# A decoder step with a dense and a gathered expert layer: six gather buffers, values through the weights' ring, and more value products of layer 1 as three float32r products

## The chip, the core and the metric

The kernel runs on one core of a Trainium2 chip. The metric is the device time in microseconds of one execution. Five engines run their own queues of instructions in order: PE (TensorE, products into PSUM), DVE (VectorE), ACT (ScalarE), POOL (GpSimd, here the issuer of gathers), and SP (SyncE, here the issuer of all other loads and stores).

## What is computed

One step of a two-layer decoder for 512 prompt tokens (four tiles of 128, called 0 to 3) and 8 sample tokens (called tile 4). Layer 0 is a gated MLP, layer 1 differential attention; each is followed by PEER, a layer of 16384 experts, which has most of the work:

```
s = einsum('thcd,hcnd->thcn', q, keys)          # 8 heads, 2 halves, 128 keys each
sv, si = top_k(s, 16)                           # then the best 16 of the 16 x 16 sums
act = gelu(einsum('thkd,td->thk', u_tab[eidx], h))
x  += einsum('thk,thkd->td', softmax(top_s) * act, v_tab[eidx])
```

So each token takes 128 rows (1024 float32 each) of the table u and 128 rows of the table v, for each of the two layers.

## The kernel before

The tokens of each layer are shared out in two ways. Two tiles are **gathered**: for each of 128 places of a token list POOL issues an indirect load of 128 rows (512 KB) into a buffer `gath` of the pool `gb` (line 706), and DVE multiplies it with h and sums (u rows, L715), or adds it, scaled, to x (v rows, L722). That is 512 gathers and 512 products of DVE per layer. The other two tiles, 256 tokens, are **dense**: `dense_peer` runs through all 16384 experts, 128 at a time, in four quarters of 32 blocks. Tiles 0 and 1 are dense in layer 0 and gathered in layer 1; 2 and 3 the other way round.

For a quarter q, `acts(q)` loads 32 blocks of u (`ub`, 512 KB each, from the ring `wt` of the pool `wp`, four buffers, which also holds all weights), and PE makes the activations W. In quarter 0 these are float32 products; later each block is split: `split` has ACT copy a rounded float32r part (`wh`, L209) and DVE make the rest (`wl`, L211), and three float32r products (hi hi, hi lo, lo hi: L488, L489, L491) take the place of one float32 product. `gates(q)` builds one-hot tiles (`ohj`, by ACT, L526 and L529, or by DVE, L520; `gi`, by DVE), has PE multiply them into `ps_g` (L533) and DVE multiply the result into W (L536), 16 times a quarter. Then the value blocks: for each of 32 blocks a load `vb` of 512 KB and PE adds W times v to four PSUM tiles y, by four float32 products (L576) or, in quarter 3 of both layers, by twelve float32r products (L572 to L574); for those v is split as above (with the tiles of `split`), and W as well (`wdh` by ACT, L565; `wdl` by DVE, L567, both in the buffers of `ohj`). The float32 blocks load v into three buffers of their own (tag `vb`), those of quarter 3 into the ring `wt`. The loop over the value blocks of quarter q draws `acts(q + 2)` (eight blocks in each of the first NV = 4 steps) and `gates(q + 1)` (in the other 28); `acts(1)` is drawn during `gates(0)`.

The order of instructions on every engine is set by a scheduler when the program is built. The products with gathered rows are held by `tick` and `pace`: the n-th may stand no earlier than the n-th of a list of named instructions of the dense work of the same layer. So gathered and dense work run side by side, through the front of a layer (projections, top 16, attention) and its dense stage. Before layer 1 goes on with tiles 2, 3, 1 and 4, the gathers of layer 0 must have ended, since tiles 2 and 3 are the gathered ones; its first part takes tile 0 alone.

`s_k` is the buffer for the scores of a tile in the first group of a layer, from which DVE ranks the 16 best.

Of the kernel before, what the change touches and what calls it, by code (L numbers as in the profile page):

```python
# [8 lines left out]
F32 = mybir.dt.float32  # L9
FR = mybir.dt.float32r  # L10
# [8 lines left out]
D = 1024  # L19
# [16 lines left out]
def body(ctx: ExitStack, tc: tile.TileContext, a):  # L36
# [3 lines left out]
    per = ctx.enter_context(tc.tile_pool(name="per", bufs=1))  # L40
    gb = ctx.enter_context(tc.tile_pool(name="gb", bufs=5))
    ks = ctx.enter_context(tc.tile_pool(name="ks", bufs=2))
    wp = ctx.enter_context(tc.tile_pool(name="wp", bufs=4))
# [425 lines left out]
    def dense_peer(layer, dpa, open_rest, open_odd, smp):  # L469
# [3 lines left out]
        NQ, QI, NV = 4, 32, 4  # L473
        J_DVE = [[1, 0, 0, 0], [1, 1, 1, 1]]
        V3 = [[3], [3]]
        W = {}
# [65 lines left out]
        dpb, py = open_rest()  # L542
# [9 lines left out]
        for q in range(NQ):  # L552
            na, ng = (na if not q else acts(q + 1), gates(q + 1)) if q + 1 < NQ else (iter(()), iter(()))
            for il in range(QI):
                i = q * QI + il
                w = W[q][:, il, :]
                r0 = layer * NE + i * 128
                three = q in V3[layer] and (il >= NV or q == NQ - 1)
                v = wp.tile([128, D], F32, name="vb", tag="wt") if three else \
                    dpa.tile([128, D], F32, name="vb", tag="vb", bufs=3)  # L560
                SY.dma_start(v, a["peer_v"][r0:r0 + 128, :])
                if three:
                    vh, vl = [z.rearrange("p c e -> p (c e)") for z in split(v.rearrange("p (c e) -> p c e", c=8), 0)]
                    wh = dpb.tile([128, 256], FR, name="wdh", tag="ohj", bufs=4)
                    SC.activation(wh, w, AF.Copy)  # L565
                    wl = dpb.tile([128, 256], FR, name="wdl", tag="ohj", bufs=4)
                    V.tensor_tensor(wl, w, wh.bitcast(F32), op=OP.subtract)  # L567
# [24 lines left out]
    def peer_front(tiles, n, layer, ph):  # L592
# [32 lines left out]
        sall = {}  # L625
# [6 lines left out]
        for sp in range(4):  # L632
# [10 lines left out]
            for t in tiles:  # L643
                c0 = col(t)
                if t < 4:
                    s = sall[t][:, sp] if sall else wk.tile([128, 4, 128], F32, name="s_k", tag="s_k", bufs=2)
                    ps = pm.tile([128, 4, 128], F32, name="ps_s", tag="mm")
# [30 lines left out]
    def sample_finish(pss, st, layer):  # L678
        state = st.pop()
        s = wk.tile([64, 1, 2, 128], F32, name="s_s", tag="s_k", bufs=2)  # L680
        for c in range(2):
# [88 lines left out]
    def run_layer(layer, setup):  # L770
# [36 lines left out]

        dpa = pool(fs, "dpa", "left", bufs=1)
        dense_peer(layer, dpa, open_rest, open_odd, st[4])
        gathers(st, layer)  # L810
        rs.close()
# [394 lines left out]
```

## Time and profile before

| | |
|---|---|
| unprofiled, median of 3 runs | 3254.13 us (3252.62 to 3262.15) |
| profiled execution | 3267.74 us, span 3266.0 us |
| PE busy | 2997.8 us, 92% of the span |
| DVE busy | 2424.0 us, 74% |
| ACT busy | 1382.3 us, 42% |
| DMA | 976.54 MB, 299 GB/s on average |

An engine's busy time is the time in which at least one of its instructions runs. PE overlaps a product with the next, so its busy time is not a measure of how well it is used. In time: layer 0's front to about 690 us (its gathers from about 190), its dense stage to 1570, layer 1's front to about 2436 (its gathers from about 1790), its dense stage to the end.

### The profile page before, as it was taken

How to read it: one execution, taken by the hardware profiler on the slowest of the kernel's cores; microseconds unless marked ns; L12 is line 12 of the kernel's file. 1: busy time of each engine (PE TensorE's matmuls, PEld its weight loads, DVE VectorE, ACT ScalarE, POOL GpSimd, SP SyncE). 2: the span in 40 equal slices, each digit the busy share in tenths (PEclk: the TensorE clock that was granted, in tenths of full speed). 3: DMA queues.
4: the chain of work that ended last, by engine and by line, in shares of the span. 5: the costliest groups of instructions: out<-in, count | busy, mean ns of one | idle time of the engine just before them, and what ended most of it. 6: DMA issues, size and time to landing. Idle time of an engine off the chain costs nothing.

```text
span 3266.0 us, 50065 instructions
## 1 busy us (share of the span) xinstructions
PE 2997.8 (92%) x18048; PEld 2237.3 (69%) x18048; DVE 2424.0 (74%) x5095; ACT 1382.3 (42%) x3156; POOL 1334.2 (41%) x1061
## 2 busy tenths in 40 slices
PE   7998979889899999978898988688799999999999
PEld 7898646788458758646787643455689658757757
DVE  1489779679776776679725788869989887686685
ACT  2344021256583593583353233321237433363444
POOL 0036662024555454455300556534334455354340
PEclk9999989999999999989999988699899999999999
DMA  7678987468999899889955989777778999989885
GB/s 247 230 280 308 336 318 244 149 225 304 386 345 365 319 350 373 313 306 373 351 168 189 361 311 324 253 266 239 284 275 308 340 364 361 328 314 355 329 306 165
DMA packets 271563, 976.54 MB, mean 299 GB/s; under 512 B 30938, under 2 KB 31770, under 8 KB 271306
## 3 DMA queue, kind: packets, MB, share of 16 engines
q0 software_dynamic: 152064, 553.72, 46.9%
q1 hardware_dynamic: 119250, 419.62, 36.1%
q8 instruction: 142, 2.33, 0.3%
q14 instruction: 107, 0.88, 0.1%
HBM read 966.76 MB, written 6.46 MB: 298 GB/s over the span
## 4 chain that ended last, share of the span: by engine, by line
PE 53%; DVE 13%; issue 12%; DMA 11%; POOL 7%; ACT 4%; another core or an unknown queue 0%; SPq 0%; POOLq 0%; DVEq 0%; ACTq 0%
PE y L576 13%; PE ps_d L231 7%; POOL gath L706 7%; PE ps_a L494 6%; PE ps_a L488 5%; PE ps_a L489 5%; PE ps_a L491 4%; DMA gath<-peer_v,ix 4%; DMA gath<-peer_u,ix 3%; PE ps_g L533 3%; DVE x L722 2%; ACT ohj L526 2%; DVE si L369 2%; DVE gath L715 2%; PE y L573 1%
## 5 line engine op out<-in xcount | busy, mean ns | idle before, releaser
L706 POOL DMA_INDIRECT gath<-peer_u,ix x512 | 651.5, 1272 | 947.4 <-DVE ix L674 355.5
L706 POOL DMA_INDIRECT gath<-peer_v,ix x512 | 644.8, 1259 | 718.2 <-DVE x L722 381.3
L722 DVE SCALAR_TENSOR_TENSOR x<-gath,act,x 128x1024 f32<-128x1024 f32 x512 | 655.6, 1281 | 70.3 <-DMA gath<-peer_v,ix 59.7
L576 PE MATMUL y<-vb,W 128*128 128x512 f32 x1536 | 703.4, 604 | 0.9 <-DMA vb<-peer_v 0.9
L715 DVE SCALAR_TENSOR_TENSOR gath<-gath,h_g 128x1024 f32<-128x1024 f32 x512 | 615.6, 1221 | 95.3 <-DMA gath<-peer_u,ix 94.0
L526 ACT ACTIVATE ohj<-iota,selJ 128x128 f16<-128x128 f32 x1408 | 426.0, 389 | 166.9 <-PE ps_g L533 152.8
L576 PEld LDWEIGHTS y<-vb,W 128*128 128x128 f32 x1536 | 283.3, 193 | 301.9 <-issue 299.2
L231 PE MATMUL ps_d<-hT,wt 128*128 128x128 f32 (+3 forms) x2048 | 433.6, 371 | 26.8 <-DMA wt<-w_in 5.9
L488 PE MATMUL ps_a<-hPh,wh 128*128 128x256 f32 x1536 | 399.5, 297 | 13.2 <-ACT wh L209 12.8
L231 PEld LDWEIGHTS ps_d<-hT,wt 128*128 128x128 f32 x2048 | 307.2, 200 | 139.2 <-issue 18.5
L211 DVE TENSOR_TENSOR wl<-ub,wh 128x1024 fp32r<-128x1024 f32 x192 | 234.9, 1224 | 205.3 <-ACT wh L209 177.7
L489 PE MATMUL ps_a<-hPl,wh 128*128 128x256 f32 x1536 | 382.2, 286 | 0.0
L209 ACT ACTIVATE wh<-ub 128x1024 fp32r<-128x1024 f32 x192 | 202.0, 1054 | 278.7 <-PE ps_a L489 243.5
L488 PEld LDWEIGHTS ps_a<-hPh,wh 128*128 128x128 f32 x1536 | 298.0, 194 | 26.3 <-ACT wh L209 14.3
L489 PEld LDWEIGHTS ps_a<-hPl,wh 128*128 128x128 f32 x1536 | 297.9, 194 | 8.9 <-issue 8.9
L494 PE MATMUL ps_a<-hT,ub 128*128 128x256 f32 x1024 | 228.2, 384 | 25.2 <-ACT W L499 25.2
L533 PEld LDWEIGHTS <-ohj 128*128 128x128 f16 x4096 | 182.3, 121 | 98.1 <-issue 55.9
L494 PEld LDWEIGHTS ps_a<-hT,ub 128*128 128x128 f32 x1024 | 196.1, 193 | 54.1 <-ACT W L499 26.0
L533 PE MATMUL ps_g<-gi,ohj 128*128 128x32 f16 x4096 | 193.0, 205 | 42.1 <-ACT ohj L529 24.6
L491 PE MATMUL ps_a<-hPh,wl 128*128 128x256 f32 x1536 | 224.4, 289 | 2.0 <-DVE wl L211 2.0
L499 ACT ACTIVATE W<-ps_a 128x256 f32<-128x256 f32 x256 | 96.0, 378 | 306.1 <-PE ps_a L491 149.3
L491 PEld LDWEIGHTS ps_a<-hPh,wl 128*128 128x128 f32 x1536 | 200.5, 193 | 9.6 <-issue 7.0
(299 smaller groups left out, 3841.9 us busy)
## 6 DMA issues: line engine op xcount, KB each, us to landing
ub<-peer_ut SPq DMA_DIRECT2D x256, 512.0 KB
vb<-peer_v SPq DMA_DIRECT2D x256, 512.0 KB
wt<-w_in SPq DMA_DIRECT2D x64, 512.0 KB
wt<-peer_wq SPq DMA_DIRECT2D x64, 512.0 KB
wt<-w_out SPq DMA_DIRECT2D x32, 512.0 KB
gath<-peer_u,ix POOLq DMA_INDIRECT x512
gath<-peer_v,ix POOLq DMA_INDIRECT x512
wt<-w_k SPq DMA_DIRECT2D x16, 512.0 KB
```

The lines of the kernel that those rows point to most:

```text
L211: tick(V.tensor_tensor(wl, w, wh.bitcast(F32), op=OP.subtract), k)
L231: z = PE.matmul(ps[:, :n], wt[:, c, :], rhs[:, c0 + c, :n], start=c0 + c == 0, stop=c0 + c == nk - 1)
L488: PE.matmul(ps, uh[:, c, :], hP[0][:, c, :], start=c == 0, stop=False)
L489: PE.matmul(ps, uh[:, c, :], hP[1][:, c, :], start=False, stop=False)
L491: PE.matmul(ps, ul[:, c, :], hP[0][:, c, :], start=False, stop=c == 7)
L494: z = PE.matmul(ps, u[:, c, :], hT[:, c, :256], start=c == 0, stop=c == 7)
L526: SC.activation(oh[:, :, k], iota128, AF.Abs, scale=-1.0, bias=selJ[:, t2 + k:t2 + k + 1])
L533: PE.matmul(ps[:, :, t - t1], oh[:, :, k], gi[:, c, (t - t0) // 2, :, t % 2], start=c == 0, stop=c == 1)
L576: PE.matmul(y[t][hf], w[:, ts], v[:, hs], start=i == 0, stop=i == 127)
L706: GP.indirect_dma_start(out=t, out_offset=None, in_=table, in_offset=bass.IndirectOffsetOnAxis(ap=ix[:, k:k + 1], axis=0))
L715: z = V.scalar_tensor_tensor(u, u, 1.0, h, op0=OP.mult, op1=OP.mult, accum_out=act[:, k:k + 1])
L722: z = V.scalar_tensor_tensor(x[t], v, act[:, k:k + 1], x[t], op0=OP.mult, op1=OP.add)
```

## The change

- The pool of gather buffers has six buffers instead of five.
- In layer 1 the value blocks of quarter 0 (all 32) and of quarters 1 and 2 (the last 28 of 32) are made by three float32r products, as those of quarter 3 are. Layer 0 keeps quarter 3 alone.
- In both layers every value block but the first four of quarters 1 and 2 loads v into the ring `wt`; the buffers `vb` go from three to one.
- `wdh` and `wdl` have two buffers each of their own, and no longer those of `ohj`.
- In layer 0 `s_k` has one buffer instead of two.

```
--- before.py
+++ after.py
@@ -38,7 +38,7 @@
     V, SC, PE, GP, SY = nc.vector, nc.scalar, nc.tensor, nc.gpsimd, nc.sync
 
     per = ctx.enter_context(tc.tile_pool(name="per", bufs=1))
-    gb = ctx.enter_context(tc.tile_pool(name="gb", bufs=5))
+    gb = ctx.enter_context(tc.tile_pool(name="gb", bufs=6))
     ks = ctx.enter_context(tc.tile_pool(name="ks", bufs=2))
     wp = ctx.enter_context(tc.tile_pool(name="wp", bufs=4))
     pt = ctx.enter_context(tc.tile_pool(name="pt", bufs=4, space=bass.MemoryType.PSUM))
@@ -472,7 +472,7 @@
         hP = [dpa.tile([128, 8, 256], FR, name=f"hP{k}") for k in "hl"]
         NQ, QI, NV = 4, 32, 4
         J_DVE = [[1, 0, 0, 0], [1, 1, 1, 1]]
-        V3 = [[3], [3]]
+        V3 = [[3], [0, 1, 2, 3]]
         W = {}
 
         def acts(q):
@@ -555,15 +555,16 @@
                 i = q * QI + il
                 w = W[q][:, il, :]
                 r0 = layer * NE + i * 128
-                three = q in V3[layer] and (il >= NV or q == NQ - 1)
-                v = wp.tile([128, D], F32, name="vb", tag="wt") if three else \
-                    dpa.tile([128, D], F32, name="vb", tag="vb", bufs=3)
+                three = q in V3[layer] and (il >= NV or q in (0, NQ - 1))
+
+                v = wp.tile([128, D], F32, name="vb", tag="wt") if il >= NV or q in (0, NQ - 1) else \
+                    dpa.tile([128, D], F32, name="vb", tag="vb", bufs=1)
                 SY.dma_start(v, a["peer_v"][r0:r0 + 128, :])
                 if three:
                     vh, vl = [z.rearrange("p c e -> p (c e)") for z in split(v.rearrange("p (c e) -> p c e", c=8), 0)]
-                    wh = dpb.tile([128, 256], FR, name="wdh", tag="ohj", bufs=4)
+                    wh = dpb.tile([128, 256], FR, name="wdh", tag="wdh", bufs=2)
                     SC.activation(wh, w, AF.Copy)
-                    wl = dpb.tile([128, 256], FR, name="wdl", tag="ohj", bufs=4)
+                    wl = dpb.tile([128, 256], FR, name="wdl", tag="wdl", bufs=2)
                     V.tensor_tensor(wl, w, wh.bitcast(F32), op=OP.subtract)
                 for t in range(2):
                     for hf in range(2):
@@ -643,7 +644,7 @@
             for t in tiles:
                 c0 = col(t)
                 if t < 4:
-                    s = sall[t][:, sp] if sall else wk.tile([128, 4, 128], F32, name="s_k", tag="s_k", bufs=2)
+                    s = sall[t][:, sp] if sall else wk.tile([128, 4, 128], F32, name="s_k", tag="s_k", bufs=1 + layer)
                     ps = pm.tile([128, 4, 128], F32, name="ps_s", tag="mm")
                     for i in range(4):
                         PE.matmul(ps[:, i, :], qT[:, o + i, c0:c0 + 128], kT[:, o + i, :], start=True, stop=True)
@@ -677,7 +678,7 @@
 
     def sample_finish(pss, st, layer):
         state = st.pop()
-        s = wk.tile([64, 1, 2, 128], F32, name="s_s", tag="s_k", bufs=2)
+        s = wk.tile([64, 1, 2, 128], F32, name="s_s", tag="s_k", bufs=1 + layer)
         for c in range(2):
             SC.activation(s[:, 0, c], pss[c], AF.Copy)
         yield from topk_rank(s, 64, 1, state, 0)
```

The scheduler orders every engine anew. Three places follow. In what follows line numbers beyond 558 are one higher after the change.

DVE in layer 1, in the gates of quarter 2, from the fourth product into W on. Before:

```order
L536 TENSOR_TENSOR W<-ps_g,W 128x32x16
L512 TENSOR_TENSOR gi<-selq,iotaP 128x1024
L520 TENSOR_TENSOR ohj<-selb,iotaJ 128x1024
L715 SCALAR_TENSOR_TENSOR gath,act<-gath,h_g 128x1024
L536 TENSOR_TENSOR W<-ps_g,W 128x32x16
L520 TENSOR_TENSOR ohj<-selb,iotaJ 128x1024
L514 TENSOR_TENSOR gi<-gi,selb 128x1024 x2
L715 SCALAR_TENSOR_TENSOR gath,act<-gath,h_g 128x1024 x2
L536 TENSOR_TENSOR W<-ps_g,W 128x32x16
```

After:

```order
L536 TENSOR_TENSOR W<-ps_g,W 128x32x16
L512 TENSOR_TENSOR gi<-selq,iotaP 128x1024
L716 SCALAR_TENSOR_TENSOR gath,act<-gath,h_g 128x1024 x2
L520 TENSOR_TENSOR ohj<-selb,iotaJ 128x1024
L536 TENSOR_TENSOR W<-ps_g,W 128x32x16
L520 TENSOR_TENSOR ohj<-selb,iotaJ 128x1024
L568 TENSOR_TENSOR wdl<-W,wdh 128x256
L514 TENSOR_TENSOR gi<-gi,selb 128x1024
L211 TENSOR_TENSOR wl<-vb,wh 128x1024
L568 TENSOR_TENSOR wdl<-W,wdh 128x256
L536 TENSOR_TENSOR W<-ps_g,W 128x32x16
```

Between the products into W the differences `wl` and `wdl` of value blocks now stand beside or in place of products with gathered rows; more of the latter stand among the u blocks of quarters 2 and 3.

DVE at the end of the dense stage of layer 0, where y is added to x (L264; x_76 and x_78 are the dense tiles, x_80 a gathered one). Before:

```order
L211 TENSOR_TENSOR wl<-vb,wh 128x1024
L715 SCALAR_TENSOR_TENSOR gath,act<-gath,h_g 128x1024
L264 SCALAR_TENSOR_TENSOR x_76<-y_4453,x_76 128x512
L264 SCALAR_TENSOR_TENSOR x_76<-y_4454,x_76 128x512
L264 SCALAR_TENSOR_TENSOR x_78<-y_4455,x_78 128x512
L264 SCALAR_TENSOR_TENSOR x_78<-y_4456,x_78 128x512
L715 SCALAR_TENSOR_TENSOR gath,act<-gath,h_g 128x1024
L1034 MEMSET hT 128x8x256
```

After:

```order
L723 SCALAR_TENSOR_TENSOR x_80<-gath,act,x_80 128x1024
L568 TENSOR_TENSOR wdl<-W,wdh 128x256
L211 TENSOR_TENSOR wl<-vb,wh 128x1024 x2
L264 SCALAR_TENSOR_TENSOR x_76<-y_4453,x_76 128x512
L264 SCALAR_TENSOR_TENSOR x_76<-y_4454,x_76 128x512
L264 SCALAR_TENSOR_TENSOR x_78<-y_4455,x_78 128x512
L264 SCALAR_TENSOR_TENSOR x_78<-y_4456,x_78 128x512
L1035 MEMSET hT 128x8x256
```

Of the 512 products with gathered rows of layer 0, 25 stood behind these additions before; now none does.

SP in the dense stage of layer 1, from its first loads of u on (`o_yp` is an output). Before:

```order
L483 DMA ub<-peer_ut 128x1024 x8
L561 DMA vb<-peer_v 128x1024 x3
L483 DMA ub<-peer_ut 128x1024 x41
L760 DMA o_yp<-x_76 128x1024
L483 DMA ub<-peer_ut 128x1024 x19
L561 DMA vb<-peer_v 128x1024 x2
L483 DMA ub<-peer_ut 128x1024
L561 DMA vb<-peer_v 128x1024
L483 DMA ub<-peer_ut 128x1024
L561 DMA vb<-peer_v 128x1024 x30
```

After:

```order
L483 DMA ub<-peer_ut 128x1024 x8
L562 DMA vb<-peer_v 128x1024
L483 DMA ub<-peer_ut 128x1024 x42
L761 DMA o_yp<-x_76 128x1024
L483 DMA ub<-peer_ut 128x1024 x14
L562 DMA vb<-peer_v 128x1024 x32
L483 DMA ub<-peer_ut 128x1024 x6
L562 DMA vb<-peer_v 128x1024
```

All 32 value blocks of quarter 0 are now asked for in one run behind the 64 u blocks of quarters 0 and 1; only one load of v (of quarter 1, into its single own buffer) goes ahead of it. Layer 0 has the same order.

## Rows read from the trace of the kernel before

**Rows 1.** The page, its first line.

```profile
span 3266.0 us, 50065 instructions
```

**Rows 2.** Windows: us; busy PE, PEld, DVE, ACT, POOL; clock, DMA share, GB/s.

```profile
0.00:190.00 190.00, 163.70 (x1296) 160.55 (x1297) 67.36 (x326) 64.41 (x154) 1.29 (x5) 0.96 0.70 232
...
190.00:510.00 320.00, 288.55 (x1331) 227.11 (x1330) 263.34 (x482) 86.02 (x159) 195.96 (x147) 0.94 0.89 321
692.20:820.80 128.60, 117.42 (x1202) 112.22 (x1201) 118.05 (x150) 93.51 (x215) 65.42 (x47) 0.97 0.86 297
1570.00:1640.00 70.00, 58.85 (x440) 55.41 (x441) 48.09 (x77) 27.93 (x85) 24.39 (x20) 0.90 0.88 330
1790.00:1900.00 110.00, 110.00 (x390) 67.28 (x389) 79.98 (x116) 29.63 (x59) 66.00 (x53) 1.00 0.96 355
1790.00:2330.00 540.00, 450.77 (x1542) 259.37 (x1541) 440.49 (x1219) 146.71 (x330) 278.86 (x221) 0.86 0.82 292
```

**Rows 3.** Windows of the dense stage of layer 1, stretches A to G.

```profile
2436.40:2579.70 143.30, 139.30 (x1309) 124.38 (x1307) 128.13 (x162) 93.25 (x207) 62.51 (x48) 0.99 0.86 304
2579.70:2709.80 130.10, 128.58 (x767) 71.17 (x764) 102.87 (x165) 50.48 (x140) 75.57 (x63) 0.97 0.97 362
2709.80:2851.50 141.70, 141.70 (x996) 119.78 (x994) 97.08 (x108) 47.37 (x76) 59.64 (x50) 1.00 0.95 351
2851.50:2928.40 76.90, 75.89 (x584) 44.73 (x581) 68.89 (x99) 51.97 (x139) 36.02 (x29) 1.00 0.86 295
2928.40:3081.60 153.20, 153.20 (x965) 120.22 (x963) 104.06 (x121) 46.17 (x74) 64.06 (x54) 1.00 0.95 355
3081.60:3158.20 76.60, 76.28 (x582) 44.73 (x579) 64.32 (x95) 47.39 (x128) 36.42 (x30) 1.00 0.87 311
3158.20:3266.00 107.80, 102.42 (x413) 76.87 (x411) 66.35 (x77) 41.72 (x62) 8.67 (x6) 0.99 0.57 188
```

**Rows 4.** Groups, DVE, 2436.4 to 3266: busy, mean ns | idle before, releasers.

```profile
L722 DVE SCALAR_TENSOR_TENSOR x<-gath,act,x 128x1024 f32<-128x1024 f32 x140 | 179.4, 1282 | 5.3 <-DMA gath<-peer_v,ix 3.6 <-DVE act L719 0.2
L715 DVE SCALAR_TENSOR_TENSOR gath<-gath,h_g 128x1024 f32<-128x1024 f32 x128 | 153.0, 1221 | 5.7 <-DMA gath<-peer_u,ix 5.5
L211 DVE TENSOR_TENSOR wl<-ub,wh 128x1024 fp32r<-128x1024 f32 x93 | 113.9, 1225 | 90.9 <-ACT wh L209 77.0 <-issue 8.4 <-ACT W L499 5.0
...
L211 DVE TENSOR_TENSOR wl<-vb,wh 128x1024 fp32r<-128x1024 f32 x32 | 39.2, 1226 | 18.7 <-ACT wh L209 18.7
...
L567 DVE TENSOR_TENSOR wdl<-W,wdh 128x256 fp32r<-128x256 f32 x32 | 13.5, 424 | 17.7 <-ACT wdh L565 17.7
```

**Rows 5.** Chain that ended last, one piece; timeline, two: start us, us.

```profile
3015.65 10.30 PE y L576 x24
...
3202.13 1.09 PE L572 MATMUL y<-wh,wdh 128*128 128x512 f32 x4
...
3204.93 1.09 PE L572 MATMUL y<-wh,wdh 128*128 128x512 f32 x4
```

**Rows 6.** Waits of DVE, 190:510, then 1790:2330: us, times, longest.

```profile
DVE gath L715 <- DMA gath<-peer_u,ix: 24.8, 26, 4.5
DVE x L722 <- DMA gath<-peer_v,ix: 20.2, 21, 2.6
...
DVE gath L715 <- DMA gath<-peer_u,ix: 42.4, 34, 6.8
DVE x L722 <- DMA gath<-peer_v,ix: 14.2, 14, 2.7
```

**Rows 7.** Windows, 20 us in the layer 0 dense stage.

```profile
1500.00:1520.00 20.00, 18.22 (x77) 13.89 (x76) 19.96 (x28) 10.59 (x16) 10.50 (x10) 1.00 1.03 416
```

**Rows 8.** Groups, ACT, 3158.2 to 3266: busy, mean ns | idle before.

```profile
L209 ACT ACTIVATE wh<-vb 128x1024 fp32r<-128x1024 f32 x30 | 31.3, 1044 | 0.0
L565 ACT ACTIVATE wdh<-W 128x256 fp32r<-128x256 f32 x32 | 13.3, 418 | 64.4 <-PE y L573 56.7 <-DVE W L536 7.7
```

**Rows 9.** Chain that ended last, one piece: start us, us.

```profile
3160.29 7.29 DMA vb<-peer_v
```

More of the change, by code (lines that the diff above doesn't have):

```diff
@@ L40, in body @@
     per = ctx.enter_context(tc.tile_pool(name="per", bufs=1))
-    gb = ctx.enter_context(tc.tile_pool(name="gb", bufs=5))
+    gb = ctx.enter_context(tc.tile_pool(name="gb", bufs=6))
     ks = ctx.enter_context(tc.tile_pool(name="ks", bufs=2))
@@ L474, in dense_peer @@
         J_DVE = [[1, 0, 0, 0], [1, 1, 1, 1]]
-        V3 = [[3], [3]]
+        V3 = [[3], [0, 1, 2, 3]]
         W = {}
@@ L557, in dense_peer @@
                 r0 = layer * NE + i * 128
-                three = q in V3[layer] and (il >= NV or q == NQ - 1)
-                v = wp.tile([128, D], F32, name="vb", tag="wt") if three else \
-                    dpa.tile([128, D], F32, name="vb", tag="vb", bufs=3)
+                three = q in V3[layer] and (il >= NV or q in (0, NQ - 1))
+                v = wp.tile([128, D], F32, name="vb", tag="wt") if il >= NV or q in (0, NQ - 1) else \
+                    dpa.tile([128, D], F32, name="vb", tag="vb", bufs=1)
                 SY.dma_start(v, a["peer_v"][r0:r0 + 128, :])
@@ L563, in dense_peer @@
                     vh, vl = [z.rearrange("p c e -> p (c e)") for z in split(v.rearrange("p (c e) -> p c e", c=8), 0)]
-                    wh = dpb.tile([128, 256], FR, name="wdh", tag="ohj", bufs=4)
+                    wh = dpb.tile([128, 256], FR, name="wdh", tag="wdh", bufs=2)
                     SC.activation(wh, w, AF.Copy)
-                    wl = dpb.tile([128, 256], FR, name="wdl", tag="ohj", bufs=4)
+                    wl = dpb.tile([128, 256], FR, name="wdl", tag="wdl", bufs=2)
                     V.tensor_tensor(wl, w, wh.bitcast(F32), op=OP.subtract)
@@ L645, in peer_front @@
                 if t < 4:
-                    s = sall[t][:, sp] if sall else wk.tile([128, 4, 128], F32, name="s_k", tag="s_k", bufs=2)
+                    s = sall[t][:, sp] if sall else wk.tile([128, 4, 128], F32, name="s_k", tag="s_k", bufs=1 + layer)
                     ps = pm.tile([128, 4, 128], F32, name="ps_s", tag="mm")
@@ L679, in sample_finish @@
         state = st.pop()
-        s = wk.tile([64, 1, 2, 128], F32, name="s_s", tag="s_k", bufs=2)
+        s = wk.tile([64, 1, 2, 128], F32, name="s_s", tag="s_k", bufs=1 + layer)
         for c in range(2):
```

## The prediction

> **What bounds the kernel now.** The page gives a span of 3266.0 us [rows 1] in an execution of 3267.74 us; the median of the three unprofiled runs is 3254.13, 13.6 us (0.4%) lower. I sum against the profiled execution and shift the result by that difference. About 0.3%, some 10 us, is what a measurement of this kernel can tell from no change.
>
> I read the table of stages first, then cut the dense stage of layer 1 at the 1st, 17th, 18th, ... product of gates into W (L536), which gives seven stretches, named here A to G in order of time [rows 3]: A holds gates(0), B, D and F the gates of quarters 1, 2, 3 beside value products, C and E the activations of quarters 2 and 3, G the values of quarter 3. In C and E the busy time of PE is the whole stretch, 141.70 of 141.70 and 153.20 of 153.20 us; over A to G it is 817.4 of 829.6, DVE 631.7. In the groups of DVE for the same time it is DVE that waits: the differences of u stood idle 77.0 us for the hi copies of ACT (which wait in turn for PE to free their buffers), the products with gathered rows of u only 5.5 for those rows [rows 4]. So this stage is bound by PE. The two fronts, 190 to 510 and 1790 to 2330 us, are mixed: DVE works 263.3 of 320 and 440.5 of 540 us, PE 288.6 and 450.8 [rows 2], and DVE waits 45.0 and 56.6 us for gathers to land [rows 6].
>
> **What the change takes from PE.** A float32 value block is 8 PE records; 24 records in a row take 10.30 us, so a block takes 3.43 [rows 5]. A block of three float32r products repeats after 2.80 us (3202.13 to 3204.93) [rows 5]. Layer 1 gets 88 more such blocks (32 of quarter 0, 28 each of 1 and 2): 88 x 0.63 = 55 us less PE.
> The page FP8 and Floating Point Precision of the Trainium skill (TensorE Precision Notes) counts four passes for true FP32 and gives the reduced form as one read truncated to FP22; three products against four passes would save a quarter, 0.86 us a block and an estimated 75 us in all. The row above saves less, since 12 products take 2.80 us; the sum goes by the row.
>
> **What it adds.** Each new block costs ACT a hi copy of v (1.044) and of W (0.418) [rows 8], 1.46 us, and DVE the two differences (1.226 and 0.424) [rows 4], 1.65 us. 88 blocks: 129 us ACT, 145 us DVE. DVE in A to G goes from 631.7 to 776.7 us, PE from 817.4 to 762. DVE becomes the fuller engine, so the saving of PE can't come through whole.
>
> **Stretch by stretch.** The orders of before and after give the instructions that stand between the same products into W. Gather products cost 1.22 (L715) and 1.28 us (L722) [rows 4], 1.25 on average. A: 46 gather products become 48, 2 value splits come, 2 u splits go, 6 float32 blocks go and two thirds of a float32r one comes: DVE 128.1+3.4 = 131.5, PE 139.3-18.7 = 120.6. B: 53 become 39, 23 splits come, 26 float32 blocks become 22.7 float32r: DVE 102.9+19 = 122, PE 128.6-25 = 104. C: 46 become 61, 8 value splits, a u split and three gate operations come; 11.75 blocks become 4 float32 and 8.7 float32r: DVE 97.1+35.6 = 132.7, PE 141.7-3 = 138.4. D: 30 become 20, 16 splits come, 15.25 blocks become 16.3: DVE 68.9+12 = 80.9, PE 75.9-7.3 = 68.6. E: 52 become 72, the splits of v go from 2 to 12, two u splits move in, 17.5 blocks become 4 and 12: DVE 104.1+44.8 = 148.9, PE 153.2-12 = 141.2. F: 30 become 20, 14 splits come, 15.5 blocks become 14: DVE 64.3+10.6 = 74.9, PE 76.3-14 = 62.3. G: 36 blocks, 4 of them float32, become 45.7 float32r: PE 102.4+24.6 = 127, its 5.4 us of end stay: 132.4; DVE 86. PE falls by 55 and DVE rises by 145, as it must. The larger of each pair adds up to 131.5+122+138.4+80.9+148.9+74.9+132.4 = 829.0. The same sum of before is 822.8, and the stage took 829.6. So on paper the stage gains nothing: what PE gives, DVE takes.
> To this comes friction, since two in-order engines that are both full lose time to each other. The row nearest to that is 692.2 to 820.8, where PE has 117.4 and DVE 118.1 us of work and 128.6 pass, 9% over the larger [rows 2]; in E, bound by one engine, it is 0. I take 3% of A to F (697 us), 21 us, between the bounds 0 and 63, because B, D and F have 15 to 17% between the engines and A 8, and only C and E (4 and 5%) are as even as that row. ACT is covered in D and F but hardly: 52.0+16.3 x 1.46 = 76 of 81 us and 47.4+20 = 68 of 75. Dense stage of layer 1: +20 us, bounds 0 and +62.
>
> **Six gather buffers.** A gather is issued one product earlier, at least 1.22 us. The waits for landings are 45.0 us in 47 times and 56.6 in 48 [rows 6], about 1 us each, so most of them can vanish. Not all lie on the path: in 1790 to 1900 PE is busy 110.0 of 110.0 us, and of the 30 us that DVE idles there [rows 2] none costs anything today; I put 23 of the 56.6 into it, which leaves 33. In 190 to 510 PE idles only 31.5 us. I take 30% of 45.0 and 60% of 33: 13+20, less 6 since transfers then come closer together (321 and 292 GB/s now [rows 2]; the fullest 20 us that I found moved 416 [rows 7]). That is -27 us, bounds 0 and -64 (all 33, and all that PE idles in the first front).
>
> **The values by the weights' ring.** In layer 0 no product changes form. SP asks for v in one run of 32 per quarter instead of single blocks between the u blocks, with one own buffer for the first four blocks of quarters 1 and 2. A single buffer makes each of those loads wait for the product before it; in the new order four or more u blocks lie between two of them, of 3.2 us each (C, 141.7 less 11.75 x 3.43, over 32 [rows 3]), more than the 7.3 us that a late v took in the chain that ended last [rows 9], so I cost it at nothing; without that cover it is 7.3 us for each of 16 blocks, 117 us. What moves in layer 0 is the gather work: of 512 products 487 stood ahead of the add of y to x, now all do. So 25 x 1.25 = 31 us of DVE leave 1570 to 1640, where DVE is busy 48.1 of 70.0 and PE only 58.9 [rows 2]. PE idles 11 us there; I take -6, bounds -11 and 0. The dense stage of layer 0 takes these 25 products in, beside fewer PE gaps from an even spread of the value blocks: 0, bounds -15 and +15. One s_k buffer instead of two in layer 0 lets the copy of one group's scores wait for the ranks of the group before; this falls into the first 190 us, where DVE works 67.4 and so has the time between two groups, and I cost it at 0; uncovered it is at most that work, 67 us.
>
> **Sum.** +20 -27 -6 +0 = -13 us: 3267.7 - 13 = 3254.7 profiled, 3241 against the median of the unprofiled runs.
>
> **The rivals.**
> *Fronts win* (chance 0.24): the waits that go are those on the path, and DVE runs through A to F nearly without gaps because gathers arrive earlier. Fronts -50, seam -8, dense +5: -53, 3201 us. For it: DVE waits 102 us for gathers in the fronts, all of one cause. Against it: PE is already 90% busy in the first.
> *The splits clog the gates* (0.26, slower): in D, F and B the order of ACT sets a hi copy of W, which waits for the product two blocks back, between the one-hot tiles of the gates; DVE does the same with its differences. Each engine then waits for the one that waits for it, and C and E, 4 to 5% apart, behave like 692.2 to 820.8. At the full 9% friction is 63 us: dense +62, fronts -20, seam -4: +38, 3292. For it: three engines over 90% in D and F. Against it: wh, wl, wdh and wdl have two buffers each, so one block of slack. It decides once friction in A to F passes 33 us, 5% of 697, when the gains of the fronts and the seam are eaten up.
> *Transfers set the pace* (0.06, slower): C and E have 15 and 20 more gathers in less PE time. At the 351 and 355 GB/s of these stretches [rows 3] C would move 49.7+8.9 = 58.6 MB in 167 us and E 54.4+10.7 = 65.1 MB in 183: +29 and +34 over the sum above, in place of friction there; 3241+63-12 = 3292. Against it: both rates belong to stretches that wait for PE, and the fullest 20 us moved 416 GB/s [rows 7], at which E takes 156.
> The page DMA: Bandwidth & Descriptors of the Trainium skill (Where 436 GB/s comes from) puts the limit of HBM to SBUF at about 358 GB/s for a core with its neighbour streaming; by that the rival above would hold nearly as it stands. The trace, at 416, does not bear it out on this one core.
> *PE's saving comes through whole* (0.02): -55 in the dense stage. It would need 777 us of DVE work in 775 us.
>
> **How the numbers follow.** The forecast, 0.42, spans -40 to +15 about -13 by the bounds of its terms: half of it faster by over 10 us, a third or more within 10, little above. With the rivals: faster 0.24+0.02+0.20 = 0.46, same 0.20+0.05 (the clogged gates at 4 to 5%) = 0.25, slower 0.29. The range 3195 to 3297 takes in the centres of the two large rivals.
>
> **What would show it.** Right: in layer 1 PE's busy time falls by some 55 us and DVE's rises by some 140; DVE's waits for ACT's hi copies shrink from 77 us to a third; PE gets idle time behind wl, wdl and wh in B to F that it doesn't have now; the last 45 blocks run at 2.80 us; waits of DVE for gathers in the fronts fall to a half. Wrong if the stretch from the first product into W of layer 1 to the end takes less than 820 us (then DVE's work overlaps better than single stretches allow), more than 895 (then ACT or the transfers bind), or if the waits for gathers in the fronts stay at 100 us, since then latency grew with the sixth buffer.

## The result

The changed kernel takes 3282.19 us (median of 7 runs, 3273.35 to 3289.60) against 3254.13 of the kernel before: ratio 1.0078, 95% interval 1.0055 to 1.0101. It is 0.8% slower; I had forecast 0.4% faster. The profiled spans, 3281.4 and 3266.0 us, lie 15.4 us apart; the unprofiled ratio stands for some 25, since the profiled execution of before was one of its longer ones [rows 1].

I cut each profile at three instructions of DVE: the first product of gates into W (L536) of each layer, and the end of the four adds of y to x (L264). That gives four stages whose sum is the span but for some 4 us (one exception is told below):

| us | front of layer 0 | dense stage 0 | seam and front of layer 1 | dense stage 1 |
|---|---|---|---|---|
| before | 691.5 | 877.3 | 866.9 | 826.5 |
| after | 685.4 | 885.3 | 841.6 | 865.3 |
| difference | -6.1 | +8.0 | -25.3 | +38.8 |

The fronts got shorter by 31.4 us and the dense stages longer by 46.8. The windows of the stretches A to G after, cut as in [rows 3] but with G up to the last add, 4 us before the span ends (us; busy us of PE, weight load, DVE, ACT and POOL; granted clock, share of DMA time, GB/s), and the whole dense stage of layer 1:

```profile
2412.20:2549.47 137.27, 128.02 (x1286) 123.44 (x1286) 128.57 (x165) 96.08 (x213) 67.68 (x48) 0.96 0.86 299
2549.47:2670.23 120.76, 107.62 (x839) 85.45 (x838) 118.53 (x189) 77.55 (x178) 69.51 (x51) 0.92 0.88 316
2670.23:2828.84 158.61, 145.95 (x1006) 129.68 (x1006) 129.91 (x153) 59.68 (x98) 85.53 (x65) 0.97 0.97 365
2828.84:2906.82 77.98, 72.10 (x667) 58.13 (x665) 77.59 (x114) 71.83 (x172) 27.12 (x19) 0.98 0.78 247
2906.82:3075.59 168.77, 147.63 (x979) 128.56 (x978) 144.76 (x172) 62.52 (x98) 105.20 (x73) 0.97 0.97 367
3075.59:3149.22 73.63, 65.91 (x651) 53.16 (x648) 71.93 (x107) 64.53 (x155) 29.80 (x19) 1.00 0.75 251
3149.22:3277.54 128.32, 127.00 (x544) 101.38 (x542) 85.15 (x103) 60.16 (x88) 4.96 (x3) 1.00 0.60 189
...
2412.20:3277.54 865.34, 794.23 (x5951) 679.80 (x5950) 756.43 (x995) 492.33 (x996) 389.81 (x277) 0.97 0.85 302
```

Against the sums I made on paper, B, D, F and G (132.2 with its end) came out within 3 us and A 6 over. C took 158.6 for 138.4 and E 168.8 for 148.9: these two, the u blocks, lie 40 us over the sums, where the forecast had 21 us of friction for A to F together. PE, once busy all through C and E, now idles 12.7 and 21.1 us there. In the whole stage it idles 71.1 us. The waits of PE in it, by line and releaser (us, times, longest):

```profile
PE y L574 <- DVE wl L211: 31.3, 24, 4.0
PE ps_a L488 <- ACT wh L209: 22.3, 16, 1.5
PE ps_a L491 <- DVE wl L211: 5.0, 3, 2.8
PE ps_y L746 <- DMA gaths<-peer_v,ixs: 4.5, 3, 2.9
```

PE waits for the copies of the splits, 58.6 us, and for no load of u or v. What such a wait is made of shows the timeline in E (start, us, engine, line, instruction, and the idle time before it with its releaser), ACT first:

```profile
3008.75 0.38 ACT L499 ACTIVATE W<-ps_a 128x256 f32<-128x256 f32 x1 [2.49 <-PE ps_a L491]
3009.03 1.05 ACT L209 ACTIVATE wh<-ub 128x1024 fp32r<-128x1024 f32 x1
...
3007.59 1.12 PE L491 MATMUL ps_a<-hPh,wl 128*128 128x256 f32 x8
3010.13 0.39 PE L488 MATMUL ps_a<-hPh,wh 128*128 128x256 f32 x1 [1.42 <-ACT wh L209]
```

ACT holds the hi copy of the next u block behind the gelu of this one, and the gelu waits for PE. So ACT stood idle for 2.49 us, and then PE for 1.42. In the value blocks it is the wait for the lo copy, which stands on DVE between products with gathered rows.

DVE's waits for gathers in the fronts are 28.1 us (190 to 510 us) and some 30 (1790 to 2306), against 45.0 and 56.6 [rows 6]:

```profile
DVE gath L716 <- DMA gath<-peer_u,ix: 18.8, 15, 4.7
DVE x L723 <- DMA gath<-peer_v,ix: 9.3, 14, 1.2
...
DVE gath L716 <- DMA gath<-peer_u,ix: 27.8, 24, 2.6
```

With five gather buffers and all else as changed (e2, below) they are 46.5 and 53.3 again, so it is the sixth buffer that shortens them.

### The profile page after: what moved, and what is told of

It is laid out like the page before. It is cut to its first block, busy times and chain, and to the rows that moved or that the text cites. A ratio compares the mean times of both kernels' runs of the same rounds, so it can differ in the third digit from the quotient of the medians.

```text
span 3281.4 us, 51491 instructions
## 1 busy us (share of the span) xinstructions
PE 2968.1 (90%) x18400; PEld 2306.8 (70%) x18400; DVE 2545.4 (78%) x5271; ACT 1496.7 (46%) x3332; POOL 1407.3 (43%) x1061
## 4 chain that ended last, share of the span: by engine, by line
PE 63%; DVE 15%; issue 7%; ACT 6%; DMA 6%; POOL 3%; SPq 0%; DVEq 0%; POOLq 0%; ACTq 0%
PE ps_d L231 11%; PE y L577 10%; PE ps_a L494 6%; PE ps_a L488 6%; PE ps_a L489 5%; PE ps_a L491 5%; PE y L574 3%; PE ps_g L533 3%; DVE gath L716 3%; PE y L575 3%; POOL gath L707 3%; PE y L573 2%; ACT ohj L526 2%; DVE wl L211 2%; ACT wh L209 2%
## 5 line engine op out<-in xcount | busy, mean ns | idle before, releaser
L707 POOL DMA_INDIRECT gath<-peer_u,ix x512 | 690.3, 1348 | 919.8 <-DVE ix L675 409.9
L707 POOL DMA_INDIRECT gath<-peer_v,ix x512 | 676.0, 1320 | 648.3 <-DVE x L723 346.7
L723 DVE SCALAR_TENSOR_TENSOR x<-gath,act,x 128x1024 f32<-128x1024 f32 x512 | 654.7, 1279 | 27.1 <-DMA gath<-peer_v,ix 22.1
L577 PE MATMUL y<-vb,W 128*128 128x512 f32 x832 | 377.4, 599 | 0.0
L574 PE MATMUL y<-wl,wdh 128*128 128x512 f32 x608 | 254.8, 420 | 33.5 <-DVE wl L211 32.1
L577 PEld LDWEIGHTS y<-vb,W 128*128 128x128 f32 x832 | 151.3, 190 | 159.0 <-issue 158.8
L575 PE MATMUL y<-wh,wdl 128*128 128x512 f32 x608 | 247.0, 407 | 0.0
```

The lines of the kernel that those rows point to most:

```text
L574: PE.matmul(y[t][hf], wh[:, ts], vl[:, hs], start=False, stop=False)
L575: PE.matmul(y[t][hf], wl[:, ts], vh[:, hs], start=False, stop=i == 127)
L577: PE.matmul(y[t][hf], w[:, ts], v[:, hs], start=i == 0, stop=i == 127)
L707: GP.indirect_dma_start(out=t, out_offset=None, in_=table, in_offset=bass.IndirectOffsetOnAxis(ap=ix[:, k:k + 1], axis=0))
L723: z = V.scalar_tensor_tensor(x[t], v, act[:, k:k + 1], x[t], op0=OP.mult, op1=OP.add)
```

## The experiments

Stages in us as above, medians unprofiled. Each group of runs had runs of before on the same chip (their medians 3254 to 3269 us), so the ratio compares, not the median. A run without a ratio was executed once. The stages are those of one profiled execution each: that of e2 was its slowest, 16 us over its median, and those of f1 and k1 lie 7 us under and 8 over theirs. So I take a difference of stages to be good to some 10 us only, and give ratios beside those that carry the argument.

| run | median us (runs) | ratio, 95% interval | front 0 | dense 0 | front 1 | dense 1 |
|---|---|---|---|---|---|---|
| e1_no_new_splits | 3285.35 (4) | 1.0091 (1.0068 to 1.0113) | 684.5 | 885.0 | 834.5 | 872.1 |
| e2_five_buffers | 3278.74 (5) | 1.0065 (1.0043 to 1.0086) | 693.9 | 854.0 | 874.6 | 866.2 |
| e3_half_products | 3259.99 (1) | | 684.4 | 887.2 | 822.4 | 860.5 |
| e4_half_gathers | 3304.30 (1) | | 685.9 | 887.0 | 859.8 | 865.7 |
| e5_six_only | 3399.56 (4) | 1.0412 (1.0385 to 1.0440) | 691.5 | 940.3 | 834.1 | 924.2 |
| f1_ring_only | 3275.55 (10) | 1.0024 (1.0008 to 1.0039) | 692.3 | 855.2 | 870.3 | 845.2 |
| f5_products_own | 3343.12 (4) | 1.0227 (1.0202 to 1.0252) | 690.6 | 881.8 | 862.7 | 905.3 |
| g1_spread16 | 3356.93 (4) | 1.0264 (1.0238 to 1.0290) | 685.5 | 959.6 | 835.3 | 873.4 |
| h1_ring_layer0 | 3244.60 (12) | 0.9969 (0.9950 to 0.9988) | 692.5 | 846.3 | 875.9 | 824.4 |
| h2_half_both | 3193.18 (1) | | 684.6 | 883.8 | 801.0 | 818.2 |
| h5_wh3 | 3247.73 (10) | 0.9979 (0.9961 to 0.9997) | 690.0 | 847.3 | 872.3 | 831.8 |
| k1_ring_wh3 | 3266.13 (10) | 1.0024 (1.0003 to 1.0046) | 697.4 | 848.0 | 879.0 | 843.9 |
| k3_wh3_wl3 | 3324.05 (4) | 1.0207 (1.0167 to 1.0246) | 719.2 | 812.9 | 922.3 | 791.9, then 71 |
| k4_ring0_wh3 | 3308.05 (1) | | 697.4 | 849.8 | 863.3 | 891.6 |
| m1_best | 3275.37 (9) | 1.0063 (1.0043 to 1.0084) | 694.3 | 848.5 | 881.2 | 841.5 |
| n1_three_no_products | 3282.40 (4) | 1.0077 (1.0050 to 1.0105) | 719.9 | 816.5 | 927.7 | 820.6 |
| n2_four_buffers | 3300.24 (1) | | 719.5 | 819.9 | 900.1 | 855.2 |

**The parts taken away from the changed kernel.**

```diff
-        V3 = [[3], [0, 1, 2, 3]]
+        V3 = [[3], [3]]
```

> The changed kernel with the float32r value products of layer 1 back to quarter 3 alone; six gather buffers, the values in the weights' ring and all other buffers stay. My theory (the loss comes from the new splits in layer 1's dense stage, which took 862.9 us from its first product into W to the add of y against 824.0 before; the fronts gained 31): the stage goes back to 824 +-6, the fronts keep their gain, so 3282 - 39 = 3243 us, ratio to before 0.993 to 1.000. Rival 'the ring is the loss' (the loads of v share four buffers with u in both layers): the dense stage stays above 840 and the kernel is no faster than before.

Without any new product the dense stage of layer 1 is no shorter (872.1, 6.8 us longer), and unprofiled the two kernels can't be told apart (1.0091 and 1.0078). The rival held: with six gather buffers the new products are not the loss.

```diff
-    gb = ctx.enter_context(tc.tile_pool(name="gb", bufs=6))
+    gb = ctx.enter_context(tc.tile_pool(name="gb", bufs=5))
```

> The changed kernel with five gather buffers, all else as changed. If the sixth buffer makes the gain of the fronts (waits of DVE for gathers fell from 101.6 to about 56 us): these waits come back to about 100 us, fronts 20 to 30 us longer, 3305 to 3312 us, ratio to before 1.015 to 1.019, layer 1's dense stage within 6 us of 862.9. Rival 'the gain comes from the gather work that moved out of the seam between the layers': waits return but the time rises by under 10 us, 3282 to 3292.

The sixth buffer takes 8.5 and 33.0 us from the fronts and gives 31.3 to the dense stage of layer 0, 0.9 less to that of layer 1. Unprofiled the kernels with six and with five can't be told apart (1.0078 and 1.0065). 33 products with gathered rows, some 41 us of DVE, have moved from the seam and front of layer 1 into dense stage 0 (360 there instead of 327). In the last quarter of layer 0, DVE then has 52 products with gathered rows instead of 41, and PE waits 17.1 us for hi copies of v instead of 7.3. SP's loads of v into the ring wait for lo copies, which DVE makes between those products, 55.9 us instead of 38.3.

**Less load.** In layer 1 the products with gathered rows over 512 of 1024 columns (e3, the diff shows that of u rows; n is 512), gathers of 512 columns (e4), and both (h2); the other half of that work is left out:

```diff
-                z = V.scalar_tensor_tensor(u, u, 1.0, h, op0=OP.mult, op1=OP.mult, accum_out=act[:, k:k + 1])
+                z = V.scalar_tensor_tensor(u[:, :n], u[:, :n], 1.0, h[:, :n], op0=OP.mult, op1=OP.mult, accum_out=act[:, k:k + 1])
```

> The changed kernel with the DVE products of gathered rows in layer 1 over 512 of their 1024 columns (half of each sum is left out, the gathers still load all): some 140 us less DVE work in the dense stage of layer 1. Theory 'DVE is full': the stage becomes bound by PE, whose busy time there is 793.5 us: 800 to 820 us instead of 862.9. Rival 'clogged order' (two buffers each for wh, wl, wdh, wdl and the order on ACT and DVE make the engines wait for each other whatever the sum of work): 840 or more. Rival 'transfers': 850 or more, and DVE's waits for gathers rise.

> The changed kernel with the gathers of layer 1 at half their bytes (512 columns of other rows; the products keep their 1024 columns and read these twice, so their values are left wrong): 134 MB less in layer 1. Theory 'DVE is full' and rival 'clogged order': the dense stage of layer 1 stays within 10 us of 862.9. Rival 'transfers set the pace': it falls by 30 us or more, above all between the gates of two quarters, where the DMA share is 0.97.

> The changed kernel; in layer 1 each gather brings 512 of 1024 columns and the products with gathered rows run over these 512 alone (both halves of the work on columns 512 to 1023 are left out). Alone, neither shortened the dense stage of layer 1 much (866 and 861 us against 865). Theory of two bounds by turns (DVE in the gates, transfers in the u blocks): without both the stage falls to 800 to 825. Rival (short waits in the order of the engines, each time for ACT's or DVE's split, which no lighter load removes): it stays over 845.

Alone neither shortens the dense stage of layer 1 by over 5 us; both together take 47 us from it. The amount of one of the two was not the bound. Each load also changes the order that the scheduler makes, so these runs can't settle more.

**The parts added to the kernel before.** First the ring alone, as in the change, with one own buffer (f1), then the ring in layer 0 alone, with three own buffers in layer 1 (h1):

```diff
-                v = wp.tile([128, D], F32, name="vb", tag="wt") if three else \
+                v = wp.tile([128, D], F32, name="vb", tag="wt") if three or not layer and (il >= NV or q == 0) else \
```

> The kernel before with one edit: the values by the weights' ring, with one own buffer. Five gather buffers, no new products. Theory of the order: the ring hands out its buffers in program order, so after some 16 u blocks with four value blocks among them 14 to 18 u blocks stand alone; dense stage of layer 1 855 to 870 us instead of 824, total 3270 to 3290. Rival (six buffers are the loss): 824 +/- 10 in that stage, total within 10 us of 3254.

> The kernel before with the values by the weights' ring in layer 0 alone; layer 1, five gather buffers and three own value buffers as before. In the run with the ring in both layers the dense stage of layer 0 took 855 us instead of 877 and that of layer 1 845 instead of 826. Theory (the ring moves value blocks from the stretches of u blocks into the gates; in layer 0 these wait for ACT, which makes the one-hot tiles, and PE has room there; in layer 1 PE has none): layer 0 855, layer 1 about 826, total 3228 to 3242. Rival (what layer 0 gains comes back later, since the gathers only move): seam and front of layer 1 or its dense stage longer by 15 or more, total 3250 to 3262.

The ring isn't free, nor neutral: it takes 22.1 us from dense stage 0 and adds 18.7 to dense stage 1. It hands out its buffers in program order, so the 32 u blocks, which had 11 to 18 value blocks among them, now have three or four, and the others move into the gates. In layer 0 ACT was the bound there. The windows of the gates of quarters 2 and 3 of layer 0, before and with the ring alone:

```profile
1116.88:1214.08 97.20, 92.10 (x639) 48.02 (x639) 73.94 (x97) 97.20 (x270) 51.20 (x41) 1.00 0.92 342
1359.78:1453.71 93.93, 74.09 (x575) 40.30 (x573) 69.07 (x98) 92.24 (x252) 47.16 (x39) 0.88 0.81 293
```

```profile
1110.55:1215.65 105.10, 105.10 (x688) 53.34 (x688) 77.75 (x100) 94.59 (x261) 56.52 (x46) 1.00 0.95 352
1336.66:1442.13 105.47, 104.98 (x688) 53.10 (x687) 75.64 (x102) 94.63 (x255) 51.91 (x43) 1.00 0.94 344
```

ACT was busy 189.4 of 191.1 us there and PE 166.2; with the ring PE fills both. In layer 1 PE was full in both kinds of stretch [rows 3], so nothing is gained and PE idles 23.0 us instead of 8.4. Of these 14.6 us 11 are its waits for hi copies of u, 8.6 of them in C and E, where it had none; before, then f1:

```profile
PE ps_a L488 <- ACT wh L209: 4.0, 2, 3.2
```

```profile
PE ps_a L488 <- ACT wh L209: 15.0, 9, 3.2
```

The -22.1 of dense stage 0 is in part a shift: it holds 327 products with gathered rows instead of 336. With the ring in layer 0 alone the gain stays (846.3, 824.4): 0.31% faster than before. Unprofiled f1 and h1, which differ by the ring in layer 1 and the number of own buffers, lie 0.55% apart, 18 us.

Then six gather buffers without the ring (e5), the products without it (f5: `wdh` and `wdl` in the buffers of `ohj`, as before), and the changed kernel with u blocks drawn over 16 value blocks instead of four (g1):

```diff
-    gb = ctx.enter_context(tc.tile_pool(name="gb", bufs=5))
+    gb = ctx.enter_context(tc.tile_pool(name="gb", bufs=6))
...
-                    dpa.tile([128, D], F32, name="vb", tag="vb", bufs=3)
+                    dpa.tile([128, D], F32, name="vb", tag="vb", bufs=2)
```

> The kernel before with six gather buffers, two own value buffers instead of three and one score buffer in layer 0; values not by the ring, no new float32r products. Theory of the order (the loss is that u blocks and value blocks no longer alternate on PE in the dense stage, whatever un-mixes them): here they alternate, one value block after one to three u blocks, so the dense stage of layer 1 takes 824 +/- 12 us and the seam with front 1 keeps its 25 us less; total 3225 to 3243. Rival (six buffers only move gather work into the dense stages, which grow by what the fronts lose): dense stage of layer 1 over 850, total 3260 to 3285.

```diff
-        V3 = [[3], [3]]
+        V3 = [[3], [0, 1, 2, 3]]
...
-                v = wp.tile([128, D], F32, name="vb", tag="wt") if three else \
+                v = wp.tile([128, D], F32, name="vb", tag="wt") if q == NQ - 1 else \
```

> The kernel before with one edit: the 88 new float32r value blocks of layer 1, with v in the three own buffers (the ring for quarter 3 only, as before). Layer 0 is in the order of before. Theory of the order: the split buffers are handed out in program order too, so 21 and 23 u blocks stand alone on PE in quarters 2 and 3; dense stage of layer 1 850 to 875 us, total 3275 to 3300. Rival (the ring alone is the loss): 815 to 835 in that stage, total 3245 to 3262. What I forecast at first for the products: 844 in that stage, 3274.

```diff
-                if il < NV:
-                    for _ in range(QI // NV):
+                if il < NA:
+                    for _ in range(QI // NA):
```

> The changed kernel with one edit: in the loop over value blocks the 32 u blocks of the quarter ahead are drawn two at each of the first 16 value blocks instead of eight at each of the first four, and the gates at the last 16. So one value block follows two u blocks again, with ring, products and six buffers kept. Theory of the order: the dense stage of layer 1 falls from 863 to 825 to 845 us; total 3240 to 3262. Rival (the splits of the new products clog DVE and ACT whatever the order): stage over 855, total over 3270; with gates in half as many value blocks it could even grow.

These three were to show that u and value blocks must alternate. My theory of the order fell: g1 and e5 alternate and are slower by 2.6 and 4.1%. In g1 the gates have half the value blocks, and PE waits 63.5 us for one-hot tiles in dense stage 0 (23.3 before). In f5 PE waits 45.9 us for `ohj`, whose buffers the parts of W take, in layer 1.

**The split buffers.** Five gather buffers and a third hi buffer, with the new products (h5) and without (k1, from f1):

```diff
-        wh = wp.tile([128, 8, 128], FR, name="wh", tag="wh", bufs=2)
+        wh = wp.tile([128, 8, 128], FR, name="wh", tag="wh", bufs=3)
```

> The changed kernel with five gather buffers and, in the room of the sixth, a third buffer for the hi copies of u and v (wh). Its control is the run with five gather buffers: dense stage of layer 1 866 us, total 3278.7. Theory of the order (PE waits 1.4 us each time ACT makes the hi copy of a u block after the gelu of the block before): with a third buffer the hi copies run further ahead, stage 835 to 850, total 3250 to 3265. Rival (transfers or DVE's amount set the pace in these stretches): within 8 us of the control.

> The kernel before with the values by the weights' ring in both layers (one own buffer), a third buffer for the hi copies (wh) and one score buffer in layer 0; no new float32r products, five gather buffers. It differs from the run with the third hi buffer and the new products by the products alone. If the products gain once the hi copies run ahead (PE 55 us less): dense stage of layer 1 840 to 850 here against 832 there, total 3258 to 3270. If they gain nothing (PE's saving is taken by DVE): 825 to 836, total 3240 to 3252.

The windows of dense stage 1 with the ring and five gather buffers: no new products and two hi buffers (f1), products and two (e2), no products and three (k1), products and three (h5):

```profile
2417.82:3263.05 845.23, 822.21 (x5599) 606.48 (x5598) 634.68 (x819) 376.49 (x820) 357.72 (x278) 0.99 0.86 310
```

```profile
2422.58:3288.82 866.24, 796.89 (x5951) 680.81 (x5950) 755.12 (x995) 491.80 (x996) 393.99 (x278) 0.96 0.85 302
```

```profile
2424.39:3268.27 843.88, 822.38 (x5600) 607.15 (x5599) 633.14 (x819) 378.28 (x819) 351.27 (x278) 0.99 0.86 310
```

```profile
2409.64:3241.48 831.84, 786.83 (x5952) 667.79 (x5951) 751.40 (x995) 494.78 (x995) 397.27 (x278) 0.98 0.87 315
```

With two hi buffers the products cost 21.0 us, though PE is busy 25.3 less; with three they gain 12.0. Unprofiled they cost 0.41% and gain 0.45% by the ratios. The third buffer alone gains 1.4. (These pairs differ in the own buffers of `wdh` and `wdl` too, which come with the products, and e2 and f1 in the score buffer of layer 0.) h5 and e2 differ by the third hi buffer alone: 34.4 us in this stage, and 0.86%, 28 us, unprofiled. PE's longest wait in the stage of e2, and its waits in h5:

```profile
PE y L574 <- DVE wl L211: 37.2, 25, 4.8
```

```profile
PE ps_a L488 <- ACT wh L209: 10.3, 8, 1.5
PE y L575 <- DVE wdl L568: 8.7, 9, 2.2
PE y L574 <- DVE wl L211: 8.2, 11, 2.1
```

So with five gather buffers the waits behind two hi buffers are what the products pay for. Most of what the third one removes is not the wait for hi copies of u that I had in mind (16.7 us in e2, 10.3 in h5) but that for lo copies in the value blocks (37.2; 8.2, with 8.7 for those of W). Next the lo buffers, with four gather buffers (k3); its two controls, without the third buffers (n2) and without the new products (n1); and all of it with five gather buffers (m1):

```diff
-    gb = ctx.enter_context(tc.tile_pool(name="gb", bufs=5))
+    gb = ctx.enter_context(tc.tile_pool(name="gb", bufs=4))
...
-        wl = wp.tile([128, 8, 128], FR, name="wl", tag="wl", bufs=2)
+        wl = wp.tile([128, 8, 128], FR, name="wl", tag="wl", bufs=3)
```

> The run with five gather buffers, third hi buffer and new products, with a third buffer for the lo copies (wl) too, and four gather buffers to make room. If the lo copies bind next (PE still waits 8 us for wl and 9 for wdl there): dense stage of layer 1 810 to 825 instead of 832; fronts 20 to 35 longer by the fourth buffer, total 3255 to 3275. If not: stage 828 to 850, total over 3270.

> The changed kernel with four gather buffers, and two hi and two lo buffers as it has. If the third split buffers made the short dense stages: layer 0 840 to 860, layer 1 850 to 870, total 3360 to 3400. If the fewer gather buffers did: 815 and 795, total 3320 to 3330.

> The run with third hi and lo buffers and four gather buffers, without the 88 new float32r value blocks. There the dense stage of layer 1 took 792 us. If PE's saving comes through once the splits run ahead: 825 to 850 here, total 3350 to 3375. If not: 790 to 805, total 3315 to 3330.

```diff
-                    dpa.tile([128, D], F32, name="vb", tag="vb", bufs=1)
...
-        HB[0], NW[0], ZB[0] = 3, GROUPS[layer][1][1], 2 + layer
+        HB[0], NW[0], ZB[0] = 2 + layer, GROUPS[layer][1][1], 2
```

> Third hi and third lo buffer, all new products, five gather buffers. Room for it comes from the last own value buffer (all values by the ring), one score buffer in both layers, two instead of three buffers each for the temporary tiles of the fronts (h in layer 0, zT in layer 1). If the split buffers are the cause: layer 0 dense 810 to 835, dense stage of layer 1 795 to 815, fronts as with five gather buffers (692 and 875) or some 10 longer by the smaller temporaries; total 3180 to 3215. If the four gather buffers were the cause: dense stages 850 and 830, total 3240 to 3270.

With four gather buffers, third hi and lo buffers cut dense stage 1 from 855.2 (n2) to 791.9 (k3). But 36 of the 268 products with gathered rows that elsewhere lie inside the stage come after it, in 71 us in which PE does nothing:

```profile
3246.30:3317.00 70.70, 0.00 (x0) 0.00 (x0) 45.58 (x54) 0.22 (x1) 40.18 (x33) 0.50 0.80 272
```

With them k3 takes 863.0 us from the start of stage 1 to the end, n2 859.0: the gain is only moved. With five buffers (m1) stage 1 is 841.5, longer than without the third lo buffer; there the u blocks wait 17.4 us for hi copies again. It also has fewer temporary tiles and no own value buffer, so what made it worse isn't told apart. Nor do n1 and k3 price the products: stage 1 is 28.7 shorter with them (820.6 to 791.9), but n1 keeps all 268 in the stage and ends it after 825.1 us, and as a whole k3 is the slower (1.0207 against 1.0077). n2 shows that four buffers by themselves shorten dense stage 0 (819.9), as its second case had it, and leave dense stage 1 long (855.2), as its first had it.

Last, h1 with a third hi buffer and two own value buffers in layer 1, to tell what made e5 so slow:

```diff
-                    dpa.tile([128, D], F32, name="vb", tag="vb", bufs=3)
+                    dpa.tile([128, D], F32, name="vb", tag="vb", bufs=2)
```

> The kernel before with the ring in layer 0 alone, a third hi buffer, two own value buffers instead of three in layer 1, and one score buffer in layer 0; five gather buffers. With two own value buffers the value blocks of layer 1 stand one by one among the u blocks, as in the run with six gather buffers and no ring, where the dense stage of layer 1 took 924 us. If the sixth gather buffer made that loss: 815 to 840 here. If the two value buffers made it: over 880.

Without a sixth gather buffer dense stage 1 is longer too, by 67.2 us against h1 (891.6, one run). That is most of the 98 of e5 against before; the rest is not explained. The third hi buffer and the one score buffer made no such loss in k1, which leaves the two own value buffers. In C of k4 PE waits for values to land, with DMA at 0.97 of its time, but that is a small part of it:

```profile
PE y L576 <- DMA vb<-peer_v: 12.0, 5, 5.8
```

## Why the prediction was wrong

Kernels that differ in little but one part price the terms (profiled us; by the profiles of e2 and f1, see above):

| part | forecast | measured | from |
|---|---|---|---|
| new products, dense stage 1 | +20 | +21.0 | e2 less f1 |
| ring, dense stage 1 | 0 | +18.7 | f1 less before |
| ring, dense stage 0 | 0 together | -22.1 | f1 less before |
| sixth buffer, dense stage 0 | with the ring | +31.3 | after less e2 |
| sixth buffer, fronts and seam | -33 | -41.5 | after less e2 |
| sixth buffer, dense stage 1 | none | -0.9 | after less e2 |

These add up to +6.5; the rest of the 15.4 is small shifts of the fronts and of dense stage 0 between before, f1 and e2 (+8.9). This is one path from before to after. On another the terms differ: in the changed kernel the products go with a dense stage 1 that is 6.8 us shorter (after less e1), and without the ring, in the buffers of `ohj`, they lengthen it by 78.8 (f5 less before). So +21.0 where I had forecast +20 is partly luck.

**The step that failed** is "The values by the weights' ring", where I wrote "so I cost it at nothing" and, of the 25 gather products that move into the dense stage of layer 0, "takes these 25 products in ... 0, bounds -15 and +15". I looked at what a single buffer delays, not at what ring order does to the mix. The late loads that I weighed don't occur (in f1 PE waits for no load of v); the ring cost 18.7 us in layer 1 all the same, outside any bound that I gave but the uncovered one of 117. I missed by 28.4 us (+15.4 for -13): this is 18.7 of it, dense stage 0 is 8.0. The 0 for layer 0 hid -22.1 and +31.3: its gates were bound by ACT, which I had not looked at, and the products taken in were not free, since lo copies, and the loads that wait for them, stand behind them.

**The fronts** were right in sum: -27 and -6 forecast, -31.4 measured, waits down by 17 and some 27 us. That most of it is a shift and not a gain I didn't see: only the 8.5 us of the first front stay, while dense stage 0 with the seam and front 1 takes 1727, 1729 and 1720 us with six, five and four buffers (after, e2, n2).

**The products** were right in size on this path and half in cause. Busy time: DVE rose by 124 us where I had said 140, PE fell by 24 where I had said 55. One part of the difference is that 0.63 us a block was too much: between n1 and k3, with mean granted clocks of 1.00 and 0.99 in the stage, PE falls by 40.6, 0.46 a block. The rest I put down to the clock: in the stretches A to E the granted clock is 0.92 to 0.98, against 0.97 to 1.00 [rows 3]. Friction isn't spread over A to F by 3%; it lies in C and E, on the splits. DVE's waits for hi copies of u fell from 77.0 to 41.3, by half and not to a third, and G ran as forecast (132.2 with its end, for 132.4). None of my signs of being wrong came up: the stage takes 869 us to the end, between 820 and 895. They didn't watch the ring.

**The rivals.** *The splits clog the gates* came nearest (3292 forecast, 3282 measured), and its mechanism, each engine waiting for one that waits for it, is the one that h5 eases. I held against it that two buffers leave one block of slack; with three, and five gather buffers, the products turn from a loss into a gain. But the place was the u blocks as much as the gates. *Transfers set the pace* forecast 167 and 183 us for C and E; they took 158.6 and 168.8 with DMA at 0.97 of its time. Against it speaks that in the whole stage PE waits for no load of u or v and DVE 4.7 us for gathers; and e4, where DMA is at 0.84 and 0.81 there, has as long a stage (865.7). But C and E of e4 took 154.0 and 155.2, so it isn't ruled out as a part. h5 can't tell: its C and E, with DMA at 0.98 and 0.97, carry fewer bytes. *Fronts win* fell: it had -50 and -8 in the fronts and the seam and +5 in the dense stage, against -31.4 there and +46.8 in the two dense stages. *PE's saving comes through whole* fell.

**Open:** without the products the sixth gather buffer, with own buffers for `wdh` and `wdl` and one score buffer, lengthens dense stage 1 by 27 (e1 less f1); with them it does not (-0.9). The orders differ in too many places to say why. Nor is the ring's price fixed: in n1, with third hi and lo buffers and four gather buffers, the stage takes 820.6 with the ring. And what makes e5 so slow is shown for the value buffers alone, and not how.

## What to carry to other kernels

Price a pool by the order in which it hands out its buffers: tiles put into a shared ring follow program order, and a scheduler can no longer fill one kind of work into the gaps of another. A stage that gets shorter because transfers are buffered deeper must be read together with its neighbours, since the same work may only have moved. When work is taken from the bound engine and given to two others as copies, count the copies' buffers before counting busy time; here, with five gather buffers, one more hi buffer decided the sign, and the kernel with the ring in layer 0 alone (0.9969) or with a third hi buffer in place of the sixth gather buffer (0.9979) beats both kernels.

## What I had not expected of the hardware

TensorE's granted clock was lower in stages with more short waits: dense stage 1 of e2, with 69.4 us of PE idle and no wait over 4.8 us, has a mean of 0.96, that of f1, with 23.0 us, 0.99. The mean lies between the two levels, 1.2 and 2.4 GHz, so for a part of the stage the products ran at the lower one. No run here has the waits without the rest of the change, so that they bring the clock down is read from such pairs, not shown.

Transfers went further than I had taken: in the u blocks of quarter 2 of layer 0 of g1 one core moved 408 GB/s for 161 us.

```profile
1026.57:1187.78 161.21, 151.27 (x919) 116.40 (x918) 134.15 (x160) 45.03 (x73) 114.24 (x81) 1.00 1.02 408
```

The page DMA: Bandwidth & Descriptors of the Trainium skill (Measured) gives 425 GB/s for one core with its neighbour idle; this row, at 408, comes near it and lies above the 358 that the page gives for each of two cores that stream.
